# Ragged self-attention on one core: batches sorted by length on chip, looped bodies per 32-row class, one batch's attention between the projections of the next

## The chip, the cores and the metric

The kernel runs on one core of a Trainium2 chip. The metric is the device time of one execution in microseconds (us), the median of several executions. A profile is one further look at one execution, and its span is a few us shorter or longer than the median. Every ratio below compares runs of the state called fast, in which no slowdown of the clock marks the run as an outlier of its kernel.

PE is TensorE's matmul side, PEld its weight loads, DVE is VectorE, ACT is ScalarE, POOL is GpSimd, SP is SyncE, which here only issues transfers.

## The reference

There are 32 batches of up to 512 rows with 512 features, 8 heads of 64. Every batch has its own length, and rows past it are zero in the output.

```python
for b in range(batch):
    seq_len = lengths[b]
    qkv = x[b, :seq_len] @ w_qkv              # 512 -> 3 * 512
    q, k, v = heads of qkv                    # 8 heads of 64
    scores = 0.125 * q @ k.T
    attn = exp(scores - max);  attn /= attn.sum(-1) + 1e-8
    output[b, :seq_len] = attn @ v            # the rest stays 0
```

The lengths are drawn between 64 and 511. The draw used here has a mean of 255. Counted in tiles of 128 rows, 4 batches need four tiles (T=4), 12 need three, 11 need two and 5 need one.

## The kernel before

A framework allocates the buffers and orders the engines. The program is fully unrolled, and every batch is computed as if it had 512 rows. Lengths enter only as masks, on V and on the denominators.

```python
def stage_qkv(b):                   # projections of batch b
    dma_x(b + 3)                    # load x three batches ahead
    ...                             # cast to f16 on DVE; 16 transposes on PE; 4 copies on ACT
    for m in range(2 * NC):         # Q and K: 8 x 4 matmuls of 512 columns
        for c in range(NC):
            nc.tensor.matmul(pq, w_r[:, c, m*P:(m+1)*P], xT[:, c, :], ...)
        nc.vector.tensor_copy(out=qkT[:, m, :], in_=pq)
    for t in range(NT):             # V: 4 x 4 matmuls of 512 columns
        ...

def stage_attn(b):
    def emit_scores(i):             # one pair of heads
        for kt in range(NT):
            for par in range(2):    # two heads, rows 0-63 and 64-127
                nc.tensor.matmul(psc[:, par, :],
                    qkT[rq:rq+64, NC + i, kt*P:(kt+1)*P], qkT[rq:rq+64, i, :], ...)
            nc.scalar.activation(out=ep[:, :, kt, :], in_=psc, func=AF.Exp, scale=scale)
    def emit_av(i):                 # 32 matmuls of 65 columns, then denominator, 1/x, product
        ...
    emit_scores(0); emit_scores(1); emit_av(0); emit_scores(2); emit_av(1)
    emit_scores(3); emit_av(2); emit_av(3)

for i in range(B + 1):
    if i < B:       stage_qkv(i)        # first all projections of batch i,
    if 1 <= i <= B: stage_attn(i - 1)   # then all attention of batch i - 1
```

The softmax here doesn't subtract the row's maximum and nothing guards it: scores larger than these inputs give would overflow.

Of the kernel before, what the change touches and what calls it, by code (L numbers as in the profile page):

```python
# [1 line left out]

# [5 lines left out]

FP32 = mybir.dt.float32  # L10
# [5 lines left out]
P = 128  # L16
NH = 8
HD = 64


@with_exitstack
def kernel(
# [10 lines left out]
    NT = MAXS // P  # L33
    NC = D // P
    assert D == NH * HD

    scale = float(HD) ** -0.5

    const = ctx.enter_context(tc.tile_pool(name="const", bufs=1))
    bx = ctx.enter_context(tc.tile_pool(name="bx", bufs=2))  # L40
    bqk = ctx.enter_context(tc.tile_pool(name="bqk", bufs=3))
    bav = ctx.enter_context(tc.tile_pool(name="bav", bufs=2))
    bo = ctx.enter_context(tc.tile_pool(name="bo", bufs=2))
    epool = ctx.enter_context(tc.tile_pool(name="ep", bufs=6))
    sml = ctx.enter_context(tc.tile_pool(name="sml", bufs=4))
    ps_a = ctx.enter_context(tc.tile_pool(name="ps_a", bufs=4, space=bass.MemoryType.PSUM))
    ps_s = ctx.enter_context(tc.tile_pool(name="ps_s", bufs=2, space=bass.MemoryType.PSUM))

    xnat = [None] * B

    def dma_x(j, first=False):
        if j < B:
            xnat[j] = bx.tile([P, NT, D], FP32, tag="x_nat", bufs=4, name="x_nat")
            nc.sync.dma_start(
                out=xnat[j], in_=x[j].rearrange("(t p) d -> p t d", p=P)
            )

    dma_x(0)
    len64 = const.tile([1, B], mybir.dt.int64)
    nc.sync.dma_start(out=len64, in_=lengths.unsqueeze(0))  # L60
    dma_x(1)
    dma_x(2)

    ident = const.tile([P, P], FP32)
    make_identity(nc, ident)
    ident_f16 = const.tile([P, P], F16)
    nc.vector.tensor_copy(out=ident_f16, in_=ident)  # L67

    w_r = const.tile([P, NC, 3 * D], F16)
    w_tmp_pool = tc.alloc_tile_pool(name="wtmp", bufs=2)  # L70
    for c in range(NC):
        w_f = w_tmp_pool.tile([P, 3 * D], FP32, tag="w_f")
        nc.sync.dma_start(out=w_f, in_=w_qkv[c * P : (c + 1) * P, :])
        nc.scalar.copy(out=w_r[:, c, :], in_=w_f)  # L74
    w_tmp_pool.release()

    len_i = len64.bitcast(I32).rearrange("p (n two) -> p n two", two=2)[:, :, 0]
    len_f1 = const.tile([1, B], FP32)
    nc.vector.tensor_copy(out=len_f1, in_=len_i)
    len_f = const.tile([P, B], FP32)  # L80
    nc.gpsimd.partition_broadcast(len_f, len_f1)  # L81

    iota_i = const.tile([P, NT], I32)
    nc.gpsimd.iota(iota_i, pattern=[[P, NT]], base=0, channel_multiplier=1)  # L84
    iota_f = const.tile([P, NT], FP32)
    nc.vector.tensor_copy(out=iota_f, in_=iota_i)  # L86

    kmask = const.tile([P, NT, B], FP32)
    nc.vector.tensor_tensor(  # L89
        out=kmask,  # L90
        in0=iota_f.unsqueeze(2).broadcast_to([P, NT, B]),
        in1=len_f.unsqueeze(1).broadcast_to([P, NT, B]),
        op=ALU.is_lt,
    )
    qbig = const.tile([P, NT, B], FP32)
    nc.vector.tensor_tensor(
        out=qbig,
        in0=iota_f.unsqueeze(2).broadcast_to([P, NT, B]),
        in1=len_f.unsqueeze(1).broadcast_to([P, NT, B]),
        op=ALU.is_ge,  # L100
    )
    nc.vector.tensor_scalar_mul(qbig, qbig, 1.0e30)

    qkT_t = [None] * B
    vaug_t = [None] * B

    def stage_qkv(b):
        dma_x(b + 3)
        x_nat = xnat[b]
        x16 = bx.tile([P, NT, D], F16, tag="x16")  # L110
        nc.vector.tensor_copy(out=x16, in_=x_nat)  # L111

        xT = bx.tile([P, NC, MAXS], F16, tag="xT")
        for c in range(NC):
            pxt = ps_a.tile([P, NT, P], F16, tag="psa")
            for t in range(NT):
                nc.tensor.transpose(  # L117
                    pxt[:, t, :], x16[:, t, c * P : (c + 1) * P], ident_f16
                )
            nc.scalar.copy(out=xT[:, c, :], in_=pxt.rearrange("p t q -> p (t q)"))  # L120

        qkT = bqk.tile([P, 2 * NC, MAXS], F16, tag="qkT")
        qkT_t[b] = qkT
        for m in range(2 * NC):
            pq = ps_a.tile([P, MAXS], FP32, tag="psa")
            for c in range(NC):
                nc.tensor.matmul(  # L127
                    pq,
                    w_r[:, c, m * P : (m + 1) * P],
                    xT[:, c, :],  # L130
                    start=(c == 0),
                    stop=(c == NC - 1),
                )
            nc.vector.tensor_copy(out=qkT[:, m, :], in_=pq)  # L134

        v_aug = bav.tile([P, NT, NH, HD + 1], F16, tag="vaug")
        vaug_t[b] = v_aug
        for t in range(NT):
            pv = ps_a.tile([P, D], FP32, tag="psa")
            for c in range(NC):  # L140
                nc.tensor.matmul(  # L141
                    pv,
                    xT[:, c, t * P : (t + 1) * P],
                    w_r[:, c, 2 * D : 3 * D],
                    start=(c == 0),
                    stop=(c == NC - 1),
                )
            nc.vector.tensor_scalar_mul(  # L148
                v_aug[:, t, :, 0:HD],
                pv.rearrange("p (h d) -> p h d", d=HD),  # L150
                kmask[:, t, b : b + 1],
            )
        nc.vector.tensor_copy(  # L153
            out=v_aug[:, :, :, HD],
            in_=kmask[:, :, b].unsqueeze(2).broadcast_to([P, NT, NH]),
        )

    def stage_attn(b):
        qkT = qkT_t[b]
        v_aug = vaug_t[b]  # L160
        out_nat = bo.tile([P, NT, D], FP32, tag="out_nat")
        etp = [None] * (NH // 2)

        def emit_scores(i):
            ep = epool.tile([P, 2, NT, MAXS], F16, tag="et")
            etp[i] = ep
            for kt in range(NT):
                psc = ps_s.tile([P, 2, MAXS], FP32, tag="pssc")
                for par in range(2):
                    rq = 64 * par  # L170
                    nc.tensor.matmul(  # L171
                        psc[:, par, :],
                        qkT[rq : rq + 64, NC + i, kt * P : (kt + 1) * P],
                        qkT[rq : rq + 64, i, :],
                        start=True,
                        stop=True,
                    )
                nc.scalar.activation(  # L178
                    out=ep[:, :, kt, :], in_=psc, func=AF.Exp, scale=scale
                )  # L180

        def emit_av(i):
            ep = etp[i]
            for qt in range(NT):
                pav = ps_a.tile([P, 2, HD + 1], FP32, tag="psa")
                for par in range(2):
                    for kt in range(NT):
                        nc.tensor.matmul(  # L188
                            pav[:, par, :],
                            ep[:, par, kt, qt * P : (qt + 1) * P],  # L190
                            v_aug[:, kt, 2 * i + par, :],
                            start=(kt == 0),
                            stop=(kt == NT - 1),
                        )
                den2 = sml.tile([P, 2], FP32, tag="den2")
                nc.vector.tensor_scalar(  # L196
                    out=den2,
                    in0=pav[:, :, HD],
                    scalar1=qbig[:, qt, b : b + 1],
                    scalar2=None,  # L200
                    op0=ALU.add,
                )
                rcp2 = sml.tile([P, 2], FP32, tag="rcp2")
                nc.vector.reciprocal(out=rcp2, in_=den2)
                nc.vector.tensor_tensor(  # L205
                    out=out_nat[:, qt, i * P : (i + 1) * P].rearrange(
                        "p (h d) -> p h d", d=HD
                    ),
                    in0=pav[:, :, 0:HD],
                    in1=rcp2.unsqueeze(2).broadcast_to([P, 2, HD]),  # L210
                    op=ALU.mult,
                )

        emit_scores(0)
        emit_scores(1)
        emit_av(0)
        emit_scores(2)
        emit_av(1)
        emit_scores(3)
        emit_av(2)  # L220
        emit_av(3)
        nc.sync.dma_start(out=out[b].rearrange("(t p) d -> p t d", p=P), in_=out_nat)

    for i in range(B + 1):
        if i < B:
            stage_qkv(i)
        if 1 <= i <= B:
            stage_attn(i - 1)


# [33 lines left out]
```

## Time and profile before

| | before |
|---|---|
| median time | 867.8 us at first (868.4 us over four runs) |
| span of the profile | 865.5 us |
| PE / DVE / ACT busy | 89% / 65% / 64% |
| mean granted clock of TensorE | 0.994 |
| one batch in the steady state | 26.0 us |

These are lines of the profile page of the kernel before: part 1 (busy us, share of the span, number of instructions), the granted clock in 40 slices (9 stands for 90% or more of full speed), and part 4, the chain of waits (who held up the end, followed back).

```profile
PE 771.8 (89%) x7168; PEld 410.7 (47%) x7168; DVE 562.0 (65%) x1990; ACT 549.9 (64%) x645; POOL 1.1 (0%) x8
...
PEclk9899999999999999999999999999999999999999
...
PE 53%; ACT 41%; issue 3%; DMA 1%; POOLq 0%; DVE 0%; ACTq 0%; POOL 0%
```

The windows view of the kernel before gives the busy time of each engine in a stretch. The rows are one whole batch, then its projections alone, then its attention.

```profile
core 0: us, PE busy (x) PEld busy (x) DVE busy (x) ACT busy (x) POOL busy (x), PEclk, DMA share, GB/s
66.10:92.10 26.00, 24.01 (x226) 12.78 (x226) 17.61 (x63) 17.03 (x21) 0.00 (x0) 1.00 0.24 84
404.00:415.00 11.00, 11.00 (x53) 4.73 (x52) 9.14 (x13) 2.52 (x4) 0.00 (x0) 1.00 0.54 178
415.10:426.00 10.90, 8.98 (x129) 5.90 (x128) 6.50 (x37) 10.84 (x12) 0.00 (x0) 1.00 0.01 2
```

The timeline of ACT in one batch shows its start, its length, and in brackets how long ACT was idle before and who released it.

```profile
415.16 11.10 ACT L178 ACTIVATE ep<-psc 128x1024 f16<-128x1024 f32 x12 [8.64 <-PE psc L171]
```

A batch has two phases. While projections run (404 to 415), PE is busy all the time and ACT then sits idle for 8.64 us. While attention runs, twelve exponentials follow each other without a break (11.10 us for 12, so 0.925 us each), and PE waits for them. Neither engine is the bottleneck throughout: PE needs about 18.7 us of its 26.0 (sum of start-to-start times: 48 matmuls and 16 score pairs of 512 columns at 0.216 us, 128 of 65 columns at 0.031, 16 transposes at 0.056), and ACT about 17. A score pair is counted as one matmul: at 414.67 us the two of a pair start 0.003 us apart, and the next pair starts 0.227 us after the first.

### The profile page before, as it was taken

How to read it: one execution, taken by the hardware profiler on the slowest of the kernel's cores; microseconds unless marked ns; L12 is line 12 of the kernel's file. 1: busy time of each engine (PE TensorE's matmuls, PEld its weight loads, DVE VectorE, ACT ScalarE, POOL GpSimd, SP SyncE). 2: the span in 40 equal slices, each digit the busy share in tenths (PEclk: the TensorE clock that was granted, in tenths of full speed). 3: DMA queues.
4: the chain of work that ended last, by engine and by line, in shares of the span. 5: the costliest groups of instructions: out<-in, count | busy, mean ns of one | idle time of the engine just before them, and what ended most of it. 6: DMA issues, size and time to landing. Idle time of an engine off the chain costs nothing.

```text
span 865.5 us, 17340 instructions
## 1 busy us (share of the span) xinstructions
PE 771.8 (89%) x7168; PEld 410.7 (47%) x7168; DVE 562.0 (65%) x1990; ACT 549.9 (64%) x645; POOL 1.1 (0%) x8
## 2 busy tenths in 40 slices
PE   2989999999999999999999999999999999998995
PEld 1344445454444444445444445444445444444453
DVE  2657666667666666666666666666766666765563
ACT  3186557766557766557756557756557756557756
POOL 0000000000000000000000000000000000000000
PEclk9899999999999999999999999999999999999999
DMA  9502322112222112332112223112222101111102
GB/s 335 199 1 98 98 98 98 54 45 98 99 98 99 53 46 98 98 99 98 51 48 99 98 98 99 50 50 98 99 98 99 49 3 50 50 49 51 40 11 98
DMA packets 34449, 71.37 MB, mean 82 GB/s; under 512 B 1090, under 2 KB 1090, under 8 KB 34370
## 3 DMA queue, kind: packets, MB, share of 16 engines
q1 hardware_dynamic: 34370, 70.26, 23.6%
q8 instruction: 56, 0.92, 0.4%
q14 instruction: 23, 0.19, 0.1%
HBM read 36.70 MB, written 33.55 MB: 81 GB/s over the span
## 4 chain that ended last, share of the span: by engine, by line
PE 53%; ACT 41%; issue 3%; DMA 1%; POOLq 0%; DVE 0%; ACTq 0%; POOL 0%
ACT ep L178 40%; PE pq L127 26%; PE pv L141 13%; PE psc L171 8%; PE pxt L117 4%; PE pav L188 2%; DMA w_f<-in_w_qkv_dram 1%; ACT w_r L74 0%; POOLq L259 0%; ACT xT L120 0%; ACTq L178 0%; ACTq L259 0%; DVE out_nat L205 0%; DVE iota_f L86 0%; DVE ident_f_95 L67 0%
## 5 line engine op out<-in xcount | busy, mean ns | idle before, releaser
L178 ACT ACTIVATE ep<-psc 128x1024 f16<-128x1024 f32 x512 | 482.1, 1068 | 281.6 <-PE psc L171 280.2
L171 PE MATMUL psc<-qkT 64*128 64x512 f16 x1024 | 230.0, 381 | 57.5 <-ACT ep L178 36.8
L127 PE MATMUL pq<-xT,w_r 128*128 128x512 f16 x1024 | 235.9, 384 | 6.4 <-ACT w_r L74 6.4
L188 PE MATMUL pav<-v_aug,ep 128*128 128x65 f16 x4096 | 206.2, 195 | 11.1 <-ACT ep L178 11.1
L134 DVE CAST qkT<-pq 128x512 f16<-128x512 f32 x256 | 173.9, 690 | 53.7 <-PE pq L127 53.5
L188 PEld LDWEIGHTS <-ep 128*128 128x128 f16 x4096 | 152.3, 97 | 116.2 <-issue 93.7
L127 PEld LDWEIGHTS <-w_r 128*128 128x128 f16 x1024 | 98.2, 99 | 127.0 <-issue 11.4
L171 PEld LDWEIGHTS <-qkT 64*128 64x128 f16 x1024 | 81.7, 93 | 96.5 <-issue 55.4
L141 PE MATMUL pv<-w_r,xT 128*128 128x512 f16 x512 | 115.7, 379 | 0.0
L148 DVE TENSOR_SCALAR v_aug<-pv,kmask 128x512 f16<-128x512 f32 x128 | 96.4, 753 | 16.0 <-PE pv L141 5.5
L120 ACT COPY xT<-pxt 128x512 f16<-128x512 f16 x128 | 67.6, 591 | 20.8 <-PE pxt L117 20.7
L141 PEld LDWEIGHTS <-xT 128*128 128x128 f16 x512 | 50.1, 98 | 60.4
L117 PE MATMUL pxt<-ident_f_95,x_129 128*128 128x128 f16 x16 | 1.9, 308 | 12.0 <-DVE ident_f_95 L67 12.0
L74 ACT CAST w_r<-w_f 128x1536 f16<-128x1536 f32 x4 | 5.9, 1480 | 4.8 <-DMA w_f<-in_w_qkv_dram 4.8
L117 PEld LDWEIGHTS <-x_129 128*128 128x128 f16 x16 | 1.7, 142 | 11.9 <-DVE x_129 L111 7.3
L153 DVE CAST v_aug<-kmask 128x32 f16<-128x32 f32 x32 | 7.0, 219 | 0.0
L111 DVE CAST x_129<-x_nat 128x2048 f16<-128x2048 f32 x1 | 1.2, 1227 | 6.0 <-DMA x_nat<-in_x_dram 6.0
L89 DVE TENSOR_TENSOR kmask<-iota_f,len_f 128x128 f32<-128x128 f32 x1 | 0.3, 293 | 4.7 <-POOL len_f L81 4.7
L86 DVE CAST iota_f<-iota_i 128x4 f32<-128x4 int32 x1 | 0.2, 247 | 4.2 <-POOL iota_i L84 4.2
L196 DVE TENSOR_SCALAR den_379<-pav,qbig 128x2 f32<-128x2 f32 x1 | 0.2, 219 | 4.1 <-PE pav L188 4.1
L111 DVE CAST x_6203<-x_nat 128x2048 f16<-128x2048 f32 x1 | 1.2, 1228 | 1.6 <-PE pxt L117 1.6
L111 DVE CAST x_8193<-x_nat 128x2048 f16<-128x2048 f32 x1 | 1.2, 1228 | 1.3 <-PE pxt L117 1.3
(1639 smaller groups left out, 447.5 us busy)
## 6 DMA issues: line engine op xcount, KB each, us to landing
x_nat<-in_x_dram SPq DMA_DIRECT2D x32, 1024.0 KB, 6.0
out_dram<-out_nat SPq DMA_DIRECT2D x32, 1024.0 KB, 5.2
w_f<-in_w_qkv_dram SPq DMA_DIRECT2D x4, 768.0 KB, 8.8
len_84<-in_lengths_dram SPq DMA_DIRECT2D x1, 0.2 KB
```

Source lines behind the costliest of these rows:

```text
L74: nc.scalar.copy(out=w_r[:, c, :], in_=w_f)
L111: nc.vector.tensor_copy(out=x16, in_=x_nat)
L117: nc.tensor.transpose(pxt[:, t, :], x16[:, t, c * P : (c + 1) * P], ident_f16)
L120: nc.scalar.copy(out=xT[:, c, :], in_=pxt.rearrange("p t q -> p (t q)"))
L127: nc.tensor.matmul(pq, w_r[:, c, m * P : (m + 1) * P], xT[:, c, :], start=(c == 0), stop=(c == NC - 1),)
L134: nc.vector.tensor_copy(out=qkT[:, m, :], in_=pq)
L141: nc.tensor.matmul(pv, xT[:, c, t * P : (t + 1) * P], w_r[:, c, 2 * D : 3 * D], start=(c == 0), stop=(c == NC - 1),)
L148: nc.vector.tensor_scalar_mul(v_aug[:, t, :, 0:HD], pv.rearrange("p (h d) -> p h d", d=HD), kmask[:, t, b : b + 1],)
L153: nc.vector.tensor_copy(out=v_aug[:, :, :, HD], in_=kmask[:, :, b].unsqueeze(2).broadcast_to([P, NT, NH]),)
L171: nc.tensor.matmul(psc[:, par, :], qkT[rq : rq + 64, NC + i, kt * P : (kt + 1) * P], qkT[rq : rq + 64, i, :], start=True, stop=True,)
L178: nc.scalar.activation(out=ep[:, :, kt, :], in_=psc, func=AF.Exp, scale=scale)
L188: nc.tensor.matmul(pav[:, par, :], ep[:, par, kt, qt * P : (qt + 1) * P], v_aug[:, kt, 2 * i + par, :], start=(kt == 0), stop=(kt == NT - 1),)
```

## The change: intent and diff

The intent is threefold. Work is done only for the rows that exist. The attention of one batch stands between the projections of the next, matmul group by matmul group, so that ACT and PE work at the same time. And the lengths stay data: the program doesn't know them when it is compiled.

For that, the framework's scheduling is replaced by five hand-written engine programs with semaphores. DVE computes each batch's rank by length. The engines read from that how many batches are longer than each multiple of 32, and each runs 15 loops, one for each class of 512, 480, ... 64 rows. A loop's body does the attention of rank r and the projections of rank r + 1 and the transposes of rank r + 2, all at the sizes of rank r, which are large enough because ranks fall.

The core of the diff, cut (`...`):

```diff
+CLASSES = [32 * k for k in range(16, 1, -1)]
+    def group(pr, b, eng, mms, evac):     # matmuls into PSUM bank b, emptied by eng
+        if b in free: acquire(pr, b)      # PE waits until the bank is free
+        pr.add("pe", ...)                 # the matmuls; the last one signals "full"
+        pr.take(eng, full[(b, eng)])
+        pr.add(eng, lambda e: evac(e).then_inc(free[b], 1))
...
+    def make_body(N):                     # T = tiles of 128 rows for N rows
+        for s in range(4):                # one pair of heads a quarter
+            if T == 4: seq = {0: "S A S Q M S K X S V", 1: "S Q S K S W A S V M X", ...}[s]
+            elif T == 3: seq = {0: "S A S Q M S K X V", 1: "S Q S A S K M V X", ...}[s]
+            else:        seq = {0: "S A QK M V X", 1: "S QK A V M X", ...}[s]
+            # S: scores of the next pair, then the exponential (banks s0, s1 in turn)
+            # A: attention times V of this pair;  Q, K, V: projections of the next rank
+            # M, X: mask and product on DVE
+                elif q == "A":
+                    if s == 0:
+                        acquire(pr, "s0")     # both score banks must have been read
+                        acquire(pr, "s1")
+                    ...
+        transposes(pr, T, ["act", "dve"])
...
+    def loops(e, regs, r, body, pre1=None):
+        for k, N in enumerate(CLASSES):
+            with e.While(lambda: e.snap(r) < e.snap(regs[k])):
+                body(e, N, r)
+                e.reg_add(r, r, 1)
...
+        def _(e):                         # POOL
+            e.memset(ep[:, 1:NPAIR], 1.0)
+            e.wait_ge(s_wv, 16)
+            e.tensor_copy(out=w_r[:, :, 2*D:3*D], in_=w_f[:, :, 2*D:3*D])...
...
-    for i in range(B + 1):
-        if i < B: stage_qkv(i)
-        if 1 <= i <= B: stage_attn(i - 1)
```

Buffers become fewer as well. Q, K, V and the probabilities have one copy each, the projections two PSUM banks in place of four.

## The prediction

> **What bounds it now.** Of the 865.5 us span, TensorE is busy 89% (page, part 1); the chain of waits is PE 53%, ACT 41%. The timeline of one period (400 to 426 us, 26.0 us per batch) shows two phases. From 404 to 415 us projections run alone: PE 11.00 of 11.00 us, ACT 2.52 (windows view), ACT idle 8.64 us. From 415 to 426 attention is ACT-bound: twelve exponentials 0.925 us apart, ACT 10.84 of 10.90 us. Start to start, a 512-column matmul takes 0.216 us (31 in 6.86 us; score pairs on two row halves share one slot), a 128-column transpose 0.056, a 65-column attention-times-V matmul 0.031. So a full batch needs about 18.7 us of PE and 17 of ACT, badly overlapped.
>
> **What the change removes.** Before, all 512 rows are computed. The drawn lengths average 255, rounded to 32 they average 270; in tiles of 128: 4 batches of four, 12 of three, 11 of two, 5 of one. Queries (Q/K, scores, exponentials) now scale with the rounded length N, keys with the tiles T. The next rank's projections stand between this one's scores, so ACT should not idle 8.64 us.
>
> **PE estimates from these durations** (32 Q/K matmuls of N columns, 16T of 128 for V, 4T score pairs, 8T*T for AV, 4T transposes[...]): T=4 17.5 to 18.8 us a body, T=3 11.0 to 12.7, T=2 6.0 to 7.6, T=1 about 3. Sums: 71, 142, 74, 15 us.
>
> **What it adds.**
> - At each body's start AV waits until the exponential just issued is out, behind the copy of the transposes: about 1.5 us (copy 0.9, exponential 0.6 to 0.8). T=4 about 78 us in all, T=3 166.
> - At T=2 DVE sets the pace, about 8.5 us a body (512-column cast 0.69 us, small operations 0.15 to 0.22): about 100 us. T=1 is a chain of handoffs, and loads queue behind 768 KB of zeros: 6.5 us each, 33.
> - Start: lengths, sort, registers, only then x. POOL's first iota came at 11.3 us before; some 20 dependent operations of 0.3 us follow, x takes 6 us to land, then POOL's cast and the projections: first body at 48 us.
> - Instruction fetch: the old PE stream came straight (0.92 MB in 56 packets of 16 KB). [...]
> - Tail: 4 us.
>
> Sum 78+166+100+33+48+30+4, about 459; I say **455 us**, range **400 to 530**. Faster by over 2%: 0.98; within 2%: 0.01; slower: 0.01.
>
> **What would show it.** PE busy about 300 us, 65 to 70% of the span; ACT busy about 210 us; DVE's share highest in the T=2 stretch; PE idle 1 to 2 us at each body's start, released by ACT; first body near 48 us; no ACT idle stretch of 8 us in T=4 bodies; PE gaps called issue at back edges and class changes. HBM reads fall from 36.7 MB to about 27, writes stay 33.5.
>
> **What would make it wrong.** Back edges that refetch every time [...]; x loads or POOL casts not keeping up at T<=2; register loads of microseconds; or the boundary wait hidden (about 410).

The sum came to 459 us, and it holds 30 us for instruction fetch; without it the rest comes to 429 us. The measured durations of the first paragraph, taken in proportion to the columns, give 70.9, 140.8, 72.1 and 14.9 us for T=4, 3, 2 and 1 (an estimate from 0.216 us for 512 columns, 0.056 for a transpose, 0.031 for 65 columns). The other terms are estimates. For those of the added work the trace of the changed kernel has: the copy 0.80 to 1.01 us (T=3 and 4), the exponential 0.65 to 1.03, the sort's small operations 0.29 to 0.38 us from start to start (16.00 to 18.27 us). The 56 packets are those of queue q8 on the page, which doesn't name the engine they are for.

## The result, and the profile after

The changed kernel takes **527.61 us** (522.27 to 529.94, 4 runs), against 868.43 us before (4 runs). The ratio is 0.6068, with a 95% interval of 0.6036 to 0.6099. Ratios are the mean time of one kernel's fast runs over the mean of the other's in the same rounds, so they are not quite the ratio of the medians. The output is correct. The time lies inside the predicted range of 400 to 530 us, close to its upper end, and 72.6 us above the 455 us that were named.

The same parts of the page of the changed kernel:

```profile
PE 409.9 (78%) x5090; PEld 275.7 (52%) x5090; DVE 284.1 (54%) x725; ACT 243.8 (46%) x299; POOL 58.9 (11%) x81
...
PEclk9999997999897998999999989998798898989899
...
ACT 0%; issue 0%; ACTq 0%
```

PE is busy 78% of the span. The clock row is no longer full of nines. The chain of waits is of no use here: it breaks off after a few us (8 pieces, from 521.08 us on). Each wait is now a semaphore instruction on the engine's sequencer and not part of the matmul (681 such instructions on PE in the trace). "PEq", "ACTq" and "DVEq" below stand for these sequencers. So the bodies have to be read from the windows and the timeline.

The windows view of the changed kernel, one row for each of three whole bodies (448 rows, 352 rows, 352 rows again):

```profile
111.85:135.07 23.22, 21.11 (x272) 12.63 (x273) 12.41 (x26) 15.69 (x17) 1.92 (x2) 1.00 0.30 90
201.89:220.25 18.36, 16.60 (x188) 10.54 (x189) 9.75 (x27) 9.88 (x13) 1.49 (x2) 0.91 0.32 103
238.57:255.43 16.86, 15.11 (x189) 9.71 (x190) 10.13 (x27) 9.88 (x13) 1.49 (x2) 1.00 0.34 109
```

The third-last column is the granted clock. The two 352-row bodies do the same work and differ by 1.50 us.

Now the terms of the prediction against the trace. A body's start is the start of its first score group, or of its first projection for one tile.

| term | predicted us | measured us |
|---|---|---|
| until the first body | 48 | 58.0 |
| 4 bodies of T=4 | 78 | 106.1 |
| 12 bodies of T=3 | 166 | 210.2 |
| 11 bodies of T=2 | 100 | 123.7 |
| 5 bodies of T=1, and the tail | 37 | 30.0 |
| instruction fetch | 30 | inside the bodies |
| sum | 459 | 528.1 |

The start explains 10 us. The bodies of T=2 to 4 took 440.0 us where 344 plus some of the 30 us were expected. Four things in the trace offer themselves.

**First, the waits at the body's start.** The timeline of the changed kernel around the start of a 352-row body, all engines:

```profile
201.90 0.32 PE L197 MATMUL psc<-qkT 64*128 64x352 f16 x1
202.36 0.76 ACT L237 ACTIVATE ep<-psc 128x704 f16<-128x704 f32 x1 [0.93 <-ACTq L35]
...
203.41 0.71 PE L197 MATMUL pav<-v_aug,ep 128*128 128x65 f16 x18 [1.19 <-PEq L35]
```

PE issues one score group (201.90), then waits 1.19 us until ACT has finished the exponential of that very group (202.36 + 0.76 = 203.12), because the attention-times-V group takes both score banks back first.

**Second, the clock.** Windows of 2 us in the same body:

```profile
202.00:204.00 2.00, 0.81 (x20) 0.61 (x18) 0.00 (x0) 0.76 (x1) 1.49 (x2) 1.00 0.40 106
204.00:206.00 2.00, 2.00 (x14) 0.79 (x11) 0.85 (x3) 1.03 (x2) 0.00 (x0) 0.71 0.38 139
206.00:208.00 2.00, 2.00 (x16) 1.52 (x13) 0.97 (x3) 0.48 (x1) 0.00 (x0) 0.50 0.62 205
```

Right after this stretch with little matmul work the clock is half for 3.4 us (from 204.82 to 208.23 us in the clock record of the trace), and the body is 1.5 us longer than its twin. Besides the 1.19 us, PE had three shorter gaps there (0.18, 0.18 and 0.71 us, from 200 us on). The twin has the same 1.19 us before its first attention-times-V group (240.09 us) and no drop. All 27 bodies with T=2 to 4 wait 1.08 to 1.87 us at that place. In 13 of them the clock drops to half between 0.9 us before and 1.4 us after the first attention-times-V group, 12 times for 3.4 us and once for 6.8. How much idle time it takes isn't shown.

**Third, gaps between matmul groups.** The PE timeline of a 352-row body at full clock:

```profile
250.31 0.32 PE L197 MATMUL psc<-qkT 64*128 64x352 f16 x2
250.57 0.77 PE L197 MATMUL pa<-xT,w_r 128*128 128x352 f16 x4
251.27 0.32 PE L197 MATMUL psc<-qkT 64*128 64x352 f16 x2
251.53 0.72 PE L197 MATMUL pav<-v_aug,ep 128*128 128x65 f16 x18
252.18 0.32 PE L197 MATMUL psc<-qkT 64*128 64x352 f16 x2
```

Only the differences of the starts tell the rate, as the durations overlap: the score pair at 250.31 lasts 0.32 us, and the next group starts 0.26 us after it. By columns (0.216 us for 512 in the kernel before), a score pair of 352 columns should take 0.149 us, but the next group starts 0.26 us later. Four Q matmuls should take 0.60 us and take 0.70, and 18 attention-times-V matmuls should take 0.56 and take 0.65. So each change between 64-row score matmuls and 128-row matmuls seems to cost about 0.1 us.

**Fourth, two holes of 4.5 us,** before the first 448-row body and before the first 384-row body. Between 512 and 448, and between 448 and 384, lies a class that no batch of this draw needs. PE at the first of them:

```profile
86.98 0.53 PE L424 MATMUL psc<-qkT 64*128 64x448 f16 x1 [4.47 <-PEq L35]
```

Here is the start of the changed kernel in the timeline of all engines, with the first transposes on PE as the last line:

```profile
3.10 10.96 DVE L62 CAST bi_f<-bi_i 32x128 f32<-32x128 int32 x1
...
3.65 10.34 POOL L699 MEMSET ep<- 128x12288 f16 x1
...
38.29 1.87 PE L397 MATMUL pa<-ident,x 128*128 128x128 f16 x16 [19.34 <-PEq L35]
```

A cast of 128 elements on DVE lasts 10.96 us, until POOL has filled the unused part of the probabilities (3.65 + 10.34 = 13.99, against 3.10 + 10.96 = 14.06), and the whole sort stands behind it.

### The profile page after: what moved, and what is told of

The parts are those of the page before. It is cut to its first block, busy times and chain, and to the rows that moved or that the text cites. A ratio compares the mean times of both kernels' runs of the same rounds, so it can differ in the third digit from the quotient of the medians.

```text
span 528.1 us, 15112 instructions
## 1 busy us (share of the span) xinstructions
PE 409.9 (78%) x5090; PEld 275.7 (52%) x5090; DVE 284.1 (54%) x725; ACT 243.8 (46%) x299; POOL 58.9 (11%) x81
## 3 DMA queue, kind: packets, MB, share of 16 engines
HBM read 27.03 MB, written 33.55 MB: 115 GB/s over the span
## 5 line engine op out<-in xcount | busy, mean ns | idle before, releaser
L237 ACT ACTIVATE ep<-psc 128x896 f16<-128x896 f32 (+5 forms) x262 | 212.2, 810 | 189.5 <-ACTq L35 187.4
L197 PE MATMUL pa<-xT,w_r 128*128 128x352 f16 (+11 forms) x1050 | 168.5, 300 | 0.8 <-PEq L35 0.6
L266 DVE CAST qkT<-pa 128x352 f16<-128x352 f32 (+5 forms) x190 | 106.0, 558 | 88.4 <-DVEq L35 86.2
L197 PEld LDWEIGHTS pa<-xT,w_r 128*128 128x128 f16 x1050 | 83.0, 102 | 54.1 <-issue 29.8
L197 PE MATMUL pav<-v_aug,ep 128*128 128x65 f16 x1768 | 78.3, 199 | 38.0 <-PEq L35 37.8
L197 PE MATMUL pa<-w_r,xT 128*128 128x128 f16 (+1 forms) x1268 | 97.0, 227 | 0.1
L197 PEld LDWEIGHTS pav<-v_aug,ep 128*128 128x128 f16 x1768 | 67.4, 101 | 53.1 <-issue 50.4
L197 PE MATMUL psc<-qkT 64*128 64x352 f16 (+11 forms) x621 | 91.5, 311 | 1.5 <-PEq L35 1.5
L197 PEld LDWEIGHTS pa<-w_r,xT 128*128 128x128 f16 x1268 | 80.1, 101 | 10.5 <-issue 5.3
L299 DVE TENSOR_TENSOR v_aug<-pa,masks 128x384 f16<-128x384 f32 (+2 forms) x112 | 59.4, 531 | 14.8 <-DVEq L35 13.0
```

The lines of the kernel that those rows point to most:

```text
L197: return lambda e: e.matmul(o, lhsT, rhs, start=start, stop=stop)
L237: lambda e: e.activation(out=dst, in_=src, func=AF.Exp, scale=scale),
L266: group(pr, b, eng, mms, lambda e: e.tensor_copy(out=dst, in_=src))
L299: lambda e: e.tensor_tensor(out=v_aug[:, 0:T, 2 * i : 2 * i + 2, 0:HD], in0=pa[:, bank, 0 : T * P].rearrange("p (t a d) -> p t a d", a=2, ...
```

## Experiments

All runs are on one core, correct unless said otherwise, and each was timed against the kernel before in three rounds. The changed kernel's own four runs spread over 7.7 us. So where a run lies some 6 to 10 us from it, the difference of the medians is uncertain by several us, and the single bodies in the profiles say more.

| run | median us | ratio to before (95%) | mean clock in the profile |
|---|---|---|---|
| changed kernel | 527.6 | 0.6068 (0.6036 to 0.6099) | 0.940 |
| e1_full | 916.4 (wrong) | 1.0565 (1.0547 to 1.0584) | 0.953 |
| e11_static | 465.5 | 0.5343 (0.5311 to 0.5374) | 0.952 |
| e3_k128 | 521.5 (wrong) | 0.6008 (0.5982 to 0.6035) | 0.949 |
| e4_sem2 | 590.8 | 0.6812 (0.6798 to 0.6827) | 0.911 |
| e5_noskip | 518.0 | 0.5985 (0.5956 to 0.6014) | 0.959 |
| e6_early | 480.0 | 0.5530 (0.5520 to 0.5540) | 0.981 |
| e7_memset | 518.1 | 0.5961 (0.5940 to 0.5981) | 0.939 |
| e9_warm | 509.3 | 0.5864 (0.5852 to 0.5877) | 0.983 |
| e2_cls128 | 535.6 | 0.6165 (0.6152 to 0.6178) | 0.963 |
| e10_start_early | 472.4 | 0.5451 (0.5432 to 0.5469) | 0.988 |
| e13_group | 461.4 | 0.5310 (0.5296 to 0.5325) | 0.981 |
| e12_group_noskip | 448.9 | 0.5171 (0.5159 to 0.5183) | 0.993 |

The theory at the outset: the gain is the lengths. The new schedule has the overlap it was built for, but loses it again at the body's starts, in changes between kinds of matmuls, and through the clock. The rivals: the gain is the overlap; the excess in the bodies is the handling of semaphores; the clock falls because of load and not because of idle time.

### e1_full: all batches through the 512-row body

```diff
             q.tensor_tensor(out=thr_f, ..., op=ALU.is_gt)   # batches longer than each class
+            q.memset(thr_f, 1.0)                            # all 32 in the first class
```

> The changed kernel with every batch sent through the 512-row body, so that nothing is saved by length (rows past a length in the first three tiles come out wrong, on purpose). Theory A: the gain is the lengths, and at full size the interleaved schedule is hardly quicker than the old 26.0 us per batch, because switches between score and projection matmuls and the wait at the body's start eat the overlap: the one 512-row body took 24.4 us without its class change, so 58 + 32 x 24.4 is about 840 us, within 5% of the kernel before. Rival B: the overlap is worth what the prediction's sums say, 18.8 + 1.5 us per body: about 710 us.

Measured: 916.4 us, outside both expectations. The bodies do what theory A said: a body at full clock takes 24.57 us (24.6 us against the 26.0 us before), far from rival B's 20.3. The 32 bodies reach to 862 us. What was not foreseen is the end of the run, in its timeline:

```profile
862.18 0.69 DVE L405 COPY xT<-pa 128x1024 f16<-128x1024 f16 x1 [0.90 <-DVEq L35]
...
905.28 0.50 PE L197 MATMUL psc<-qkT 64*128 64x128 f16 x6 [43.24 <-PEq L35]
```

Between the last 512-row body and the one-tile class, the engines pass eleven loops that run zero times, and PE stands still for 43.24 us: 3.9 us for each empty class. That is the missing part. So at equal work and full clock the interleaving is worth 26.0 - 24.57 = 1.4 us per batch. Some bodies of this run, too, were 1.5 us longer, at a lower clock: with these the mean is 25.1 us. This is the worth of the interleaving as it was written, with the wait at the body's start: in e12_group_noskip below, the 512-row body takes 23.26 us.

### e11_static: the old schedule, with the lengths as constants

The kernel before, its order of work unchanged, with loops and slices cut to each batch's T and N:

```diff
-        for t in range(NT):
+        for t in range(T):          # T, N from this draw's lengths, as constants
...
-                        qkT[rq : rq + 64, i, :],
+                        qkT[rq : rq + 64, i, 0:N],
...
-        nc.sync.dma_start(out=out[b]..., in_=out_nat)
+        nc.sync.dma_start(out=out[b, 0 : T * P]..., in_=out_nat[:, 0:T, :])
+        if T < NT: nc.sync.dma_start(out=out[b, T * P :]..., in_=zero tile)
```

Unwritten columns of K and of the probabilities are filled on POOL.

> The kernel before, its schedule and order kept, with this draw's lengths built in as constants: rows cut to the length rounded to 32, tiles of 128 past it left out, their rows written from a zero tile. Theory A (lengths are all of the gain, and the sort, the loops and the new interleaving bring none beyond them): 430 to 490 us, faster than the changed kernel. Rival B (the old two-phase schedule loses much more than the new one also on short batches): 560 us or more.

Measured: 465.5 us, as theory A has it. It isn't a kernel that could be used for other lengths, and it spares the sort and the loops as well. But it shows that the lengths alone, on the old two-phase schedule, bring 403 us, and the changed kernel brought 341. One of the four runs was slow and is not in the ratio. The profile fell on that one, so nothing is read from it.

### e3_k128: scores over 128 rows

```diff
-                        qkT[rq : rq + HD, 2 * j + 1, kt * P : (kt + 1) * P],
-                        qkT[rq : rq + HD, 2 * j, 0:N],
+                        qkT[:, 2 * j + 1, kt * P : (kt + 1) * P],
+                        qkT[:, 2 * j, 0:N],
```

> The changed kernel with score matmuls over 128 rows instead of two halves of 64 (wrong scores, on purpose; the same number of matmuls and columns, but the two of a pair can no longer share a slot). Theory S: PE loses about 0.2 us per score group by the change between 64-row and 128-row matmuls, some 250 groups, 50 us in all; without it the doubled score time [...] is paid back: 505 to 540 us, and PE busy of a 448-row body stays near 21 to 22 us. Rival W (no such loss; the excess is semaphore handling on PE's sequencer or the clock): about 570 us.

Measured: 521.5 us. The score matmuls of a pair now run one after the other (0.15 us from start to start at 254.47 us, where the changed kernel has 0.003 us at 250.31) and cost PE twice the time, 41 us more in all by columns (an estimate from 0.216 us for 512), and yet the kernel is no slower. The PE timeline of this run, a 352-row body:

```profile
250.35 0.46 PE L197 MATMUL psc<-qkT 128*128 128x352 f16 x2
250.65 0.71 PE L197 MATMUL pav<-v_aug,ep 128*128 128x65 f16 x18
251.20 0.46 PE L197 MATMUL psc<-qkT 128*128 128x352 f16 x2
251.50 0.76 PE L197 MATMUL pa<-xT,w_r 128*128 128x352 f16 x4
252.09 0.83 PE L197 MATMUL pa<-w_r,xT 128*128 128x128 f16 x12
```

Two score matmuls now take 0.30 us (2 x 0.149), 18 of attention times V 0.55, four of Q 0.59: the 0.1 us at each change are gone. A 352-row body at full clock takes 16.40 us, and 16.86 in the changed kernel. With 12 score groups of 0.149 us more each, that is (0.46 + 12 x 0.149) / 12 = 0.19 us per score group for the two changes around it. A 448-row body gives (23.22 - 23.05 + 16 x 0.189) / 16 = 0.20 us. The bodies hold 4 x 16 + 12 x 12 + 11 x 4 = 252 score groups: about 50 us, an estimate worked out from these. (The 44 groups at T=2 were not measured this way. The same sum for 160-row and 224-row bodies at full clock gives 0.13 to 0.20 us, so the total may be nearer 46 us.) The prediction had counted columns only.

The weight loads (PEld) show where. This is all engines' timeline of the changed kernel at one score group, and then that of this run:

```profile
251.27 0.10 PEld L197 LDWEIGHTS psc<-qkT 64*128 64x128 f16 x2 [0.29 <-issue]
251.27 0.32 PE L197 MATMUL psc<-qkT 64*128 64x352 f16 x2
...
251.52 0.14 PEld L197 LDWEIGHTS pav<-v_aug,ep 128*128 128x128 f16 x3 [0.16 <-issue]
```

```profile
250.21 0.25 PEld L197 LDWEIGHTS psc<-qkT 128*128 128x128 f16 x2
...
250.35 0.46 PE L197 MATMUL psc<-qkT 128*128 128x352 f16 x2
250.50 0.73 PEld L197 LDWEIGHTS pav<-v_aug,ep 128*128 128x128 f16 x18
250.65 0.71 PE L197 MATMUL pav<-v_aug,ep 128*128 128x65 f16 x18
```

In the changed kernel the load of the score weights starts with its matmul, and that of the next group as late. With 128 rows everywhere the load starts 0.14 to 0.15 us ahead, behind the running matmul. So the 64-row loads, whose rows overlap with those of the 128-row matmul in flight, don't run ahead (251.27 and 251.27 us), while the 128-row loads of this run, whose rows overlap as well, do (250.21 and 250.35 us). What holds the loads at a change of rows isn't shown. The run shows the cost (0.19 to 0.20 us per score group) and that it goes with the change of rows.

### e4_sem2: more semaphore instructions on PE

```diff
         def pe(e):
+            e.nop().then_inc(s_dum, 1)
+            e.wait_ge(s_dum, 1)
+            e.nop().then_inc(s_dum, -1)      # wait and decrement become one instruction
             for k, mm in enumerate(mms):
```

> The changed kernel with two more semaphore instructions on PE's sequencer before every group of matmuls (about three times as many). Theory S (switches): under 10 us more, up to 540 us. Rival W (each semaphore instruction on PE costs about 0.1 us of matmul time): 50 us or more, 580 us and up.

Measured: 590.8 us, 63 us more. By the total, my expectation failed and the rival's number came in. The trace doesn't bear out the rival's mechanism. This is PE in a 352-row body of this run, at full clock:

```profile
305.04 0.77 PE L201 MATMUL pa<-xT,w_r 128*128 128x352 f16 x4
305.74 0.32 PE L201 MATMUL psc<-qkT 64*128 64x352 f16 x2
306.00 0.71 PE L201 MATMUL pav<-v_aug,ep 128*128 128x65 f16 x18
306.65 0.32 PE L201 MATMUL psc<-qkT 64*128 64x352 f16 x2
```

Four Q matmuls take 0.70 us from start to start, the score pair 0.26, attention times V 0.65: the same as in the changed kernel, with two more instructions before each group. So here the added instructions are hidden, and the 0.1 us at a change of rows is not their doing. The run is longer elsewhere. In the 448-row body at full clock (24.64 us against 23.22) the added time stands at four places, 0.25 to 0.65 us each: at the body's start, from the last transposes to the next body, and before two attention-times-V groups where PE waits for a moment. At T=2, too, about half of the groups lose nothing (a 160-row body grows from 9.47 to 10.87 us). And the clock is low more often: (1 - clock) times the length, summed over the bodies of T=2 to 4, is 51.2 us against 30.7 in the changed kernel. So about 20 of the 63 us can be the clock.

The run executes 734 groups (34 in a body of T=4, 30 at T=3, 17 at T=2, 6 at T=1, and the start). Dividing gives 63.2 / (2 x 734) = 0.043 us per added instruction, but that is an average over many groups that lose nothing, some that lose 0.25 us or more, and the clock, and it can't be carried over to the instructions that the changed kernel already has. Each added wait also waits for an increment issued just before it, which the existing ones don't. Taking those away was not tried, since each one guards a bank.

### e5_noskip: no empty classes

```diff
         for k, N in enumerate(CLASSES):
+            if N in (480, 416, 64):
+                continue
```

> The changed kernel without the loops of the classes 480, 416 and 64, which no batch of this draw needs. Theory F (jumping over an empty class waits for instructions that were not fetched): the two gaps of about 4.5 us before the first 448-row and the first 384-row body fall to the 0.5 us of an ordinary class change, and the time falls by 8 to 10 us, to about 518 us. Rival (those gaps are a wait for data or for another engine at a class change): no change beyond 3 us.

Measured: 518.0 us, 9.6 us less, as expected of theory F. The bodies before the two class changes shrink from 28.97 to 24.96 us and from 29.07 to 25.20 us. These two are 4.0 and 3.9 us; the rest of the 9.6 us lies within the spread of the changed kernel's runs and in a different clock. Bodies of the same class follow each other without such a hole, so the loop's own back edge costs almost nothing (in the changed kernel PE is idle 0.20 to 0.28 us before a T=3 body of the same class as the last). What costs is the jump over code that was not run. No timeline shows the fetch of instructions, but the traces' records of the DMA queues do. The page counts the pieces of 16 KB that queue q8 moved as "instruction": 21 in the changed kernel, 17 in this run. In the changed kernel one piece starts in each hole, at 83.73 and at 160.70 us. In e1_full none starts from 77 to 863 us, while the same body goes round, and 16 start between 863 and 906 us, in the long gap, where no engine is busy. A piece takes 0.95 to 1.48 us in the changed kernel, so it doesn't fill a hole of 4 us by itself. What the remainder is made of isn't shown.

### e6_early: the wait at the body's start moved

```diff
+                if s == 0:
+                    acquire(pr, "s0")        # before the first score group of the body
+                    acquire(pr, "s1")
                 for q in seq.split():
...
                         if s == 0:
-                            acquire(pr, "s0")
-                            acquire(pr, "s1")
                             if T == 2:
                                 acquire(pr, "a1")
```

The banks must be read before attention times V may use the probabilities of the body before. They have been by then. Asking after the first score group means to wait for that group's exponential in addition.

> The changed kernel with the wait for both score banks moved ahead of the first score group of a body, so that the attention-times-V matmuls wait for the exponentials of the body before and not for the one just issued. Theory B (the wait of 1.1 to 1.9 us at each of 27 body starts is on the critical path and also lets the clock drop): time 485 to 505 us, granted clock 0.96 or more, no gap over 0.5 us before the first attention-times-V group. Rival (the wait only moves on to the projections, which need the copies of the transposes): 520 us or more, clock as before.

Measured: 480.0 us, 47.6 us less, more than expected. PE at the start of a 352-row body in this run:

```profile
194.11 0.31 PE L424 MATMUL psc<-qkT 64*128 64x352 f16 x1 [0.86 <-PEq L35]
194.12 0.32 PE L197 MATMUL psc<-qkT 64*128 64x352 f16 x1
194.37 0.72 PE L197 MATMUL pav<-v_aug,ep 128*128 128x65 f16 x18
```

Attention times V now starts 0.25 us after the score group, and the clock is 1.00 in both 352-row bodies compared above (15.78 and 15.76 us, no more 18.36 and 16.86). The bodies of T=3 fall from 210.2 to 189.5 us in sum, those of T=2 from 123.7 to 98.9, those of T=4 from 106.1 to 99.2. The four runs lie within 0.5 us of each other, those of the changed kernel within 7.7.

### e9_warm: needless matmuls in the wait

```diff
                         if s == 0:
-                            acquire(pr, "s0")
                             acquire(pr, "s1")
+                            pr.add("pe", lambda e: [e.matmul(psc[:, 1, 0, 0:P], ident, ident,
+                                start=True, stop=True) for _ in range(20)])
+                            acquire(pr, "s0")
```

> The changed kernel with 20 needless 128-column matmuls in the wait at the body's start (into the score bank that is free then; about 1.1 us of a wait of 1.1 to 1.9). Theory C (some bodies take 1.4 to 1.6 us longer because the granted clock drops to about half for one stretch after idle time of PE; over all bodies some 22 us): granted clock 0.97 or more, equal bodies equally long, 505 to 518 us although each body's work is larger. Rival (the drops come of load, not of idle time): clock 0.94 or lower, 525 us or more.

Measured: 509.3 us, 18 us less, with more work. Windows of the two 352-row bodies:

```profile
201.93:218.68 16.75, 16.17 (x208) 10.81 (x209) 9.76 (x27) 9.88 (x13) 1.49 (x2) 1.00 0.35 113
235.41:252.15 16.74, 16.18 (x208) 10.81 (x209) 10.16 (x27) 9.88 (x14) 1.49 (x2) 1.00 0.34 110
```

Both are at full clock and equally long. The wait is still there: a body takes as long as the quick twin of the changed kernel. So this drop of the clock comes from idle time of PE, and it cost about 18 us of the 72.6 by the medians. By the profiles, the bodies of T=2 to 4 are 22 us shorter, while the first one starts 2.3 us later. The other 29 us of e6_early, by subtraction, are the wait itself.

### e7_memset: POOL's fill behind the sort

```diff
+            e.wait_ge(s_srt, 1)
             e.memset(ep[:, 1:NPAIR], 1.0)
```

> The changed kernel with POOL's fill of the probabilities (10.3 us) moved behind the sort. Theory P (the 128-element cast of VectorE, 10.96 us long, was held by that fill, and the whole sort with it): that cast takes 0.2 us, the sort is done at about 11 us and not 21, the first body starts at about 48 us and not 58, the time falls by 9 to 11 us. Rival (the cast waits for the lengths or the weights, or the loads of x hide it): the first body starts within 2 us of 58.

Measured: 518.1 us, 9.5 us less. The timeline of this run, all engines:

```profile
3.10 0.68 DVE L62 CAST bi_f<-bi_i 32x128 f32<-32x128 int32 x1
...
13.00 10.34 POOL L700 MEMSET ep<- 128x12288 f16 x1 [9.30 <-DVEq L69]
13.03 0.20 DVE L62 COPY n_s<-pav 128x36 f32<-128x36 f32 x1 [0.24 <-DVEq L54]
13.38 10.00 DVE L62 TENSOR_SCALAR n_k<-n_s 128x36 f32<-128x36 f32 x1
```

The cast of 128 elements takes 0.68 us (and 0.52 us of these another, shorter fill runs on POOL). The long fill now meets another small DVE instruction, SBUF to SBUF, and holds it for 10.00 us. An instruction that reads PSUM (13.03) passes in 0.20 us beside it. The first body starts at 49.9 us. So the fill holds the small instruction up, and the trace shows the size: the instruction waits for the whole fill, not for a share of it (13.38 + 10.00 = 23.38 us, and the fill ends at 13.00 + 10.34 = 23.34). By what means the fill holds it isn't shown.

### e2_cls128: four classes of 128 rows

```diff
-CLASSES = [32 * k for k in range(16, 1, -1)]
+CLASSES = [128 * k for k in range(4, 0, -1)]     # thresholds accordingly
```

> The changed kernel with four classes of 128 rows in place of fifteen of 32. By PE columns alone the coarser rounding adds 26 us (3.8 in the four-tile bodies, 10.5 in three, 10.1 in two, 1.4 in one), and it saves the two jumps over empty classes (9 us) and some ordinary class changes (about 0.5 us each): about 540 us. Theory: the tiles of 128, not the 32-row classes, carry the gain. Rival (work goes with the rounded length, mean 270 against 316 rows): 590 us or more.

Measured: 535.6 us, 8 us more than the fifteen classes, near the 540 expected. In this kernel the 32-row rounding is worth little. Of the 26 us of columns that were counted (an estimate from the measured 0.216 us for 512 columns), 8 go on the two holes, and ordinary class changes at T=3 take some 0.3 to 0.5 us each (in the changed kernel PE is idle 0.55 to 0.73 us before the first 352-, 320- and 288-row body, against 0.20 to 0.28 between equal ones). The profiles also differ in the clock (0.963 here, 0.940 there), so the 8 us aren't the rounding alone.

### e10_start_early, e13_group, e12_group_noskip: all of it together

e10 is e6 and e7 plus an earlier load of the V weights and loads of x ahead of the register reads. e13 adds pairs of score groups, for instance:

```diff
-  T=4: 1: "S Q S K S W A S V M X"     T=3: 1: "S Q S A S K M V X"
+  T=4: 1: "S S Q K S S W A V M X"     T=3: 1: "S S Q A S K M V X"
```

e12 is e13 without the three empty classes, so for this draw only.

> The wait of the early run (480.0 us) kept, and the start shortened as well: the fill of the probabilities behind the sort (9.4 us in its own run), the V weights loaded at once and not after the sort, the first loads of x issued before the class ends are read into registers (15 reads took 5.3 us). If these are on the critical path and independent of the body: first body at about 42 us, 460 to 466 us. If the weight casts of VectorE, now held by the fill, take their place: 470 us or more.

Measured: 472.4 us, 7.6 us less than e6 where 14 to 20 were hoped for. The rival's reading holds. DVE in the start of this run:

```profile
13.32 10.00 DVE L62 TENSOR_SCALAR n_k<-n_s 128x36 f32<-128x36 f32 x1
23.47 1.80 DVE L62 TENSOR_TENSOR masks<-row_f,n_k 128x132 f32<-128x132 f32 x1
```

x arrived sooner, but DVE didn't. The masks, which are needed only later, stand ahead of the weight casts, are held by the fill (10.00 us) and then run into POOL's casts (1.80 and 1.75 us in place of 0.30). After the weight casts DVE still reads its 15 registers (4.72 us idle), and copies its half of the first transposes only at 33.64 us, where ACT had its half at 28.31. The first body starts at 51.3 us and not at 42.

> The same, and the score groups of three- and four-tile bodies issued in pairs, which takes away 8 of 16 changes between score and other matmuls in a four-tile body and 4 of 12 in a three-tile body, at some 0.2 us each: 16 us. Theory S (the change costs that much on PE): 444 to 452 us. Rival (PE then waits for the exponentials, as two score groups want both banks at once): no gain over the run before it.

Measured: 461.4 us, 11 us less than e10, of 16 expected. The bodies of T=3 give what was expected (189.5 to 179.8 us, 0.2 us for each change removed). Those of T=4 give only 1.7 us of 6.4: a new wait for a score bank (0.44 us) appears, and the wait of the last transposes for their bank grows from 0.67 to 1.07 us.

> The same, without the loops of the classes that this draw doesn't need (valid for this draw alone): 8 to 10 us less than the run before it, 435 to 443 us, and below the static kernel's 465.5 us.

Measured: 448.9 us, 12.5 us less than e13 where 8 to 10 were expected, so above the 435 to 443 that were named only because e13 was, and below the static kernel's 465.5. It is the fastest, 14.9% quicker than the changed kernel, but holds for this draw. Of those that work for any lengths, e13_group is the fastest, 12.5% quicker than the changed kernel.

## Why the prediction was right or wrong

**The direction and the range were right: 527.6 us, inside 400 to 530.** That the range held is partly luck: its end is 2.4 us away, the highest of the four runs took 529.94, and two costs that the sum didn't have, the switches and the clock, make up most of the 72.6 us. The mechanism named for the gain, work by length, was right too. e11_static gets more than the whole gain from it alone. HBM reads fell to 27.03 MB as forecast, writes stayed (33.55 MB).

**"ACT should not idle 8.64 us": right, and worth little.** Its longest wait in the bodies was below 6 us, at an empty class. e1_full shows that the interleaving brings 1.4 us per full batch, and not the 5 to 6 us of the sums (2.7 us in e12_group_noskip, with the wait moved and the groups paired). ACT was busy 243.8 us, where about 210 were predicted.

**The step that failed in size is "PE estimates from these durations": 71, 142 and 74 us of PE for T=4, 3, 2.** PE was busy 88.7, 187.3 and 98.5 us in these bodies (predicted over all: about 300 us, measured 409.9). The sum took matmul rates from long runs of equal matmuls, and the new schedule consists of short runs of different ones. The missing term is the change between 64-row and 128-row matmuls, 0.19 to 0.20 us per score group at T=3 and 4, about 50 us in 252 groups (e3_k128, and e13_group at T=3). Busy time also holds the stretches at half clock: at T=2 it falls from 98.5 to 87.6 us in e6_early, at full clock. In the kernel before the same changes occur, but in its ACT-bound phase, where PE waits anyway (415.1 to 426 us: ACT busy 10.84 us of 10.90, PE 8.98).

**The clock was taken as full.** It was not: 18 to 22 us (e9_warm). The prediction named PE's idle time at each body's start, but not this consequence.

**The wait at each body's start: named and sized right for T=3 and 4.** Predicted 1.5 us, "released by ACT", measured 1.1 to 1.9 us. For T=2 the sum held none. Its removal was worth more than itself, because of the clock (47.6 us for e6_early, of which about 18 the clock).

**"At T=2 DVE sets the pace": wrong.** DVE was busy 70.8 us of 123.7 there. With the same DVE work the bodies took 98.9 us in e6_early, where PE was busy 87.6 us. The wait and the clock are what e6_early took away, and PE sets the pace of what is left. That 98.9 is near the predicted 100 is chance.

**Instruction fetch, 30 us in the sum: mis-sized, and in another place.** Two jumps over empty classes cost about 4 us each (8.0 us in the bodies of T=4, 9.6 by the medians, e5_noskip), ordinary class changes at T=3 about 0.3 to 0.5 us, back edges nearly nothing (PE idle 0.20 to 0.28 us at T=3). The warned-of "back edges that refetch every time" did not occur.

**The start, 48 us: 58.0 us, by another cause than named.** "POOL's first iota came at 11.3 us before" was carried over. It came at 1.05 us. About as much was lost all the same, as POOL's fill held a DVE cast by some 10 us (e7_memset moved the first body 8.1 us forward). So these two errors cancel, and the excess of 10 us lies in the rest of the chain, 47 us (58.0 - 1.05 - 10.3) where 37 were predicted (48 - 11.3). No run takes that rest apart.

**T=1: 6.5 us each expected, 4.5 us measured.** The loads behind the zeros arrived in time (3.4 us from issue to landing, the median of five). Such a load, issued 1.08 us after the zeros (500.08 and 499.00 us), landed 0.6 us after them (4.2 and 4.7 us from issue).

Open: the bodies of T=2 to 4 took 96 us more than the 344 of the prediction. Switches (46 to 50), clock (18 to 22) and empty classes (8) are 72 to 80 of these, if they simply add, which no run shows. Of the rest, the wait at the body's start at T=2, which the predicted 100 us didn't hold, can be 12.6 us: the bodies there take 111.5 us in e9_warm, with the wait, and 98.9 in e6_early, without it, both at full clock. What the existing semaphore instructions on PE cost stays open. e4_sem2 shows that two more of them cost nothing between most groups, and something where PE waits.

## What to carry to other kernels

Cost a fine interleaving of unlike matmuls by a measured change-over, not by the rates of long runs. And look where a "bank free" wait stands: asking one group too late made PE wait for an exponential that nobody needed (1.08 to 1.87 us), and around that wait the clock fell to half in 13 of the 27 bodies, for 3.4 us in 12 of them. Before you charge a lost time to added instructions, compare the same groups in both timelines, as a total can hide that most groups lose nothing. When a kernel gains from doing less work, measure the old schedule with less work before crediting the new one.
